# Seven block products for eight in two of eight pairs of the retention's projections

## The chip, the cores and the metric

The kernel runs on one core of one Trainium2 chip. The metric is device time in microseconds (us) of one execution. The kernel is compared with itself before one change.

## The reference

A trunk of two layers works on x of 256 positions by 2048 features, in float32. Layer 0 mixes with retention (8 heads), layer 1 with latent attention (16 heads); each is followed by a SwiGLU block of width 5632. Cut to what the change touches:

```
h    = rms_norm(x, norm_mix_pre[0])
proj = h @ ret_w_in                      # 2048 x 12288
q, k, v, g = split(proj, [2048, 4096, 8192])
q, k = rope(q), rope(k) * 256**-0.5      # 8 heads of 256
y    = retention(q, k, v)                # per head: (q k^T * decay) v
out  = silu(g) * group_norm(y) * gn_g    # 8 heads of 512
x    = x + rms_norm(out @ ret_w_out, norm_mix_post[0])
```

## The kernel before

**Tiles and products.** The 256 positions are two tiles of 128 (t = 0, 1). A projection is cut into groups of 1024 output columns, two halves of 512 (c = 0, 1), and its 2048 inputs into 16 slices of 128 (kt = 0 to 15). A group fills four PSUM banks b00, b01, b10, b11 (t, c). Each operand is kept as a high part (the value rounded to the fast matmul type) and a low part (the rest), and a product of two blocks is three matmuls of 128x128 by 512 columns: high by high, high by low, low by high. A slice of weights is loaded by one DMA of 512 KB (`raw`, 4 buffers); ScalarE casts the high part (L202), VectorE subtracts for the low part (L203), each 1024 wide (`whi`, `wlo`, 5 buffers each). PE may run at most as far as these buffers are filled.

**Sevens.** A pair p is the two slices 2p and 2p+1: a 2 by 2 block of inputs times a 2 by 2 block of weights, eight block products, 24 matmuls. For pairs in a list `sevens`, `group` forms them with seven products, 21 matmuls (Winograd's form of Strassen's method). That takes four sums of left blocks (`left_sums`, L229, formed once and used by all groups), four sums of weight blocks per group (`right_sums`, L237, tiles `ta` and `tb` with their own high and low parts `tahi`, `talo`, `tbhi`, `tblo`), and four more banks m1, m5, m6, m7. m1 and m6 come from the six banks for products, m5 and m7 are the two `misc` banks, which transposes, scores and head outputs also use. They gather over all pairs of the list. After the last such pair `combine` (L330) forms sums of them, and `add` (L341) adds these to the four banks, between the matmuls of later slices. Before the change, the gate/up groups (`gu`), the down projections (`dn`) and the retention's output projection (`rto`) have sevens.

**The retention.** Four query/key groups (rqk0 to rqk3, two heads each) are followed by eight value/gate groups (rvg0 to rvg7, one head each), all on the left operand `hT`, which `norm_piece` (L431) forms while rqk0 runs. After an rqk group VectorE turns the result (16 `rope` operations), PE transposes it (`rtp`) and forms scores (`rsc`), which VectorE multiplies with the decay (`pr`). After an rvg group the values are split (`vh`, `vl`); during the next group PE forms the head's output in a misc bank (`ry`, 3 matmuls for the first tile and 6 for the second), VectorE normalises it into `z` (L724 to L735), PE transposes z (`ztp`) and ScalarE writes it away (`yT`).

**What sets the order.** `later(k, fn)` puts work k steps ahead; a step is the load of one slice. Within that a scheduler orders the instructions of each engine; each engine then runs its own list in that order. Lists and waits are fixed when the program is built.

Of the kernel before, what the change touches and what calls it, by code (L numbers as in the profile page):

```python
# [8 lines left out]
F32 = mybir.dt.float32  # L9
F32R = mybir.dt.float32r  # L10
# [45 lines left out]
def trunk(  # L56
# [73 lines left out]
    def later(k, fn):  # L130
        order[0] += 1
        todo.append((steps[0] + k, order[0], fn))
# [125 lines left out]
    def group(  # L258
# [71 lines left out]
        def combine():  # L330
            def kept(n):
                return wp.tile([P, 512], F32, tag="mv", bufs=3, name=f"{name}_mv{n}")

            m1, u, v = kept(0), kept(1), kept(2)
            nc.scalar.copy(out=m1, in_=ms[1])
            nc.vector.tensor_add(out=u, in0=ms[6], in1=m1)
            nc.vector.tensor_add(out=v, in0=ms[7], in1=u)
            nc.vector.tensor_sub(out=u, in0=ms[5], in1=u)
            parts.update(m1=m1, u=u, v=v)

        def add(t, c):  # L341
            m1, u, v = parts["m1"], parts["u"], parts["v"]
            if (t, c) == (1, 1):
                nc.vector.tensor_sub(out=v, in0=ms[5], in1=v)
            src = {(0, 0): m1, (0, 1): u, (1, 0): v, (1, 1): v}[t, c]
            nc.vector.tensor_tensor(out=banks[t][c], in0=banks[t][c], in1=src, op=ALU.add)

        def adds(t):
# [57 lines left out]
    def tile_load(w, g, name, halves=0):  # L406

        def load(kt, first_half=False):  # L410
            n = 512 if kt < halves or first_half else 1024

            def dma(raw):
                for a in range(0, 1024, 512 if kt < halves else 1024):
                    m = 512 if kt < halves else 1024
                    nc.sync.dma_start(out=raw[:, a : a + m], in_=w[g, kt, :, a : a + m])

            parts = [(a, n, None) for a in range(0, 512 if first_half else 1024, n)]
            return weights(dma, parts, f"{name}_w{kt}")

        return load
# [5 lines left out]
    PIECES = ((0, 2), (2, 2), (4, 4), (8, 4), (12, 4))  # L427

    watch = [None]

    def norm_piece(t, i, ssq, col):  # L431
        k0, n = PIECES[i]
# [159 lines left out]
    def retention():  # L592
        first = [small(len(PIECES), "nxt", 4, f"first{t}") for t in range(NT)]

        def load_x(c, t):
            nc.sync.dma_start(
                out=xs[:, t, c * 512 : (c + 1) * 512], in_=xv[:, t, c * 512 : (c + 1) * 512]
            )

        def load_constants():  # L600
            nc.sync.dma_start(out=pos_i, in_=pos)
            nc.sync.dma_start(out=cst[:, 0:C_ID], in_=consts[:, 0:C_ID])
            nc.sync.dma_start(out=cst[:, C_MASK:C_DEC], in_=consts[:, C_MASK:C_DEC])

        load_x(0, 0)
        later(0, lambda: norm_piece(0, 0, first[0], G_MIX))
        later(0, lambda: norm_piece(0, 1, first[0], G_MIX))
# [11 lines left out]
        def qk_group(gq):  # L619
            name = f"rqk{gq}"  # L620
            return group(
                h_lhs, DT, tile_load(ret_qk, gq, name, 0 if gq else 1), name, lead=2 if gq else 3
            )

        def vg_group(h):
            name = f"rvg{h}"
            return group(h_lhs, DT, tile_load(ret_vg, h, name), name)

        with tc.tile_pool(name="rt_s", bufs=1) as sp:
            scores = {}  # L630
# [79 lines left out]
            with tc.tile_pool(name="rt_v", bufs=1) as rp:  # L710
                yT = rp.tile([P, RH * 4, NT, P], F32, name="yT")

                def mixed(h, t, pr, v, sg):
                    y = misc_bank(f"ry{h}{t}")

                    terms = [
                        (pr[a][:, (kb + t) * P : (kb + t + 1) * P], v[b][:, kb, :])
                        for kb in range(t + 1)
                        for a, b in ((0, 0), (0, 1), (1, 0))
                    ]  # L720
                    for n, (left, right) in enumerate(terms):
                        nc.tensor.matmul(y, left, right, start=n == 0, stop=n == len(terms) - 1)  # L722
                    st = rp.tile([P, 6], F32, tag="bst", bufs=4, name="bst")
                    nc.vector.bn_stats(out=st, in_=y)  # L724
                    mv = rp.tile([P, 2], F32, tag="bmv", bufs=4, name="bmv")
                    nc.vector.bn_aggr(out=mv, in_=st)
                    ve = rp.tile([P, 1], F32, tag="bve", bufs=4, name="bve")
                    nc.vector.tensor_scalar(ve, mv[:, 1:2], scalar1=EPS, scalar2=None, op0=ALU.add)
                    rs = rsqrt(ve, 1, "grs", 4, "grs")
                    z = rp.tile([P, RV], F32, tag="z", bufs=2, name="z")  # L730
                    nc.vector.scalar_tensor_tensor(
                        out=z, in0=y, scalar=mv[:, 0:1], in1=sg[:, t, :],
                        op0=ALU.subtract, op1=ALU.mult,
                    )
                    nc.vector.tensor_scalar(z, z, scalar1=rs, scalar2=None, op0=ALU.mult)  # L735

                    def transposes():
                        tp = misc_bank(f"ztp{h}{t}")
                        for j in range(4):
                            nc.tensor.transpose(  # L740
                                tp[:, j * P : (j + 1) * P], z[:, j * P : (j + 1) * P], ident
                            )
                        for j in range(4):
                            nc.scalar.activation(
                                out=yT[:, h * 4 + j, t, :], in_=tp[:, j * P : (j + 1) * P], func=AF.Copy,
                                scale=gain(G_GN, h * 4 + j),
                            )

                    later(4, transposes)

                for h in range(RH):
                    if h:
                        banks = vg_group(h)
                    vh = rp.tile([P, NT, RV], F32R, tag="vh", bufs=1, name=f"vh{h}")
                    vl = rp.tile([P, NT, RV], F32R, tag="vl", bufs=1, name=f"vl{h}")
                    ph = rp.tile([P, 3 * P], F32R, tag="ph", bufs=1, name=f"ph{h}")
                    pl = rp.tile([P, 3 * P], F32R, tag="pl", bufs=1, name=f"pl{h}")
                    split(ph, pl, scores[h])
                    sg = rp.tile([P, NT, RV], F32, tag="sg", bufs=1, name=f"sg{h}")
                    for t in range(NT):  # L760
                        split(vh[:, t, :], vl[:, t, :], banks[t][0], rx[t])
                        nc.scalar.activation(
                            out=sg[:, t, :], in_=banks[t][1], func=AF.Silu, scale=rx[t]
                        )
                    for t in range(NT):
                        later(2 + t, lambda h=h, t=t, pr=(ph, pl), v=(vh, vl), sg=sg: mixed(h, t, pr, v, sg))

                def sums():
                    both = ("vh", "vl")[sums.n % 2]
                    sums.n += 1  # L770
                    s = rp.tile([P, 2, 4, P], F32R, tag=both, bufs=1, name="rs")
                    f = rp.tile([P, 4, P], F32, tag="sg", bufs=1, name="rsf")
                    return f, s[:, 0], s[:, 1]

                sums.n = 0
                closing(
                    lambda k0, n: yT[:, k0 : k0 + n], RH * 4, ret_out, g_mix_post[0], G_FFN, "rto",
                    sevens=RTO_SEVENS, sums=sums,
                )


    def swiglu(i):
        with tc.tile_pool(name=f"ff{i}", bufs=1) as fp:
# [7 lines left out]
                    out=aT[:, j * 4 : j * 4 + 4, t, :], in_=tp.rearrange("p (j q) -> p j q", j=4)  # L791
                )


            ins = {}
            held = {}

            def sums(n=0):
                f = fp.tile([P, 4, P], F32, tag="sf", bufs=2, name=f"sf{i}")
                if n < 2:  # L800
                    hi = fp.tile([P, 4, P], F32R, tag="sa", bufs=4, name=f"sh{i}")
                    lo = fp.tile([P, 4, P], F32R, tag="sa", bufs=4, name=f"sl{i}")
                else:
                    hi = wp.tile([P, 4, P], F32R, tag="ah", bufs=3, name=f"sh{i}")
                    lo = wp.tile([P, 4, P], F32R, tag="al", bufs=3, name=f"sl{i}")
                return f, hi, lo

            def seen(t, k0, n, part):
                for p in GU_SEVENS:
                    if k0 <= 2 * p < k0 + n:  # L810
                        held[t, p] = part[:, 2 * p - k0], part[:, 2 * p - k0 + 1]
                        if (1 - t, p) in held:
                            f, hi, lo = sums(len(ins))
                            left_sums(*held[0, p], *held[1, p], f, hi, lo)
                            ins[p] = hi, lo
# [392 lines left out]
```

## Time and profile before

| | us |
|---|---|
| median of 3 runs | 2439.79 |
| lowest and highest run | 2439.47 to 2440.51 |
| the profiled execution | 2439.43 |
| its span, first to last instruction | 2437.6 |
| PE busy in it | 2425.1 |
| VectorE (DVE) busy | 1944.2 |
| ScalarE (ACT) busy | 1367.8 |

Times in the rows are microseconds from the span's start unless marked ns. PE is TensorE's matmuls, PEld its weight loads, DVE VectorE, ACT ScalarE, POOL GpSimd. A row's `x48` counts instructions. Buffer numbers are left out of names, so rvg_w_lo stands for the low parts of all value/gate groups.

### The profile page before, as it was taken

The numbers are of one execution on the slowest core, as the hardware profiler recorded it, in microseconds if no ns is written. First come the engines' busy times: TensorE is split into PE (matmuls) and PEld (weight loads), VectorE is DVE, ScalarE is ACT, GpSimd is POOL, SyncE is SP. The second block draws the span as 40 slices with busy tenths as digits, with TensorE's granted clock in tenths as the row PEclk, the third lists the DMA queues.
The fourth block names the chain that finished last, engine by engine and source line by source line (L and its number), as shares of the span: only waits on it lengthen the run. The fifth ranks groups of instructions, "written<-read, shape, count | busy, mean of one in ns | idle before, by whom it ended". The sixth has DMA issues, their size and how long they took to land.

```text
span 2437.6 us, 30634 instructions
## 1 busy us (share of the span) xinstructions
PE 2425.1 (99%) x11038; PEld 2005.3 (82%) x11038; DVE 1944.2 (80%) x2635; ACT 1367.8 (56%) x1825; POOL 25.0 (1%) x38
## 2 busy tenths in 40 slices
PE   9999999999999999999999999999999999999998
PEld 7888888888888888888888888888888888888887
DVE  7655555557888898898989997876789888899997
ACT  5433544445656555555566666655566555556664
POOL 0000000000000000000000000000000000000000
PEclk9999999999999999999999999999999999999999
DMA  7555555555656566565666565445556656566665
GB/s 263 180 185 182 180 182 180 181 179 178 200 199 201 179 200 209 188 207 181 209 199 206 193 212 160 131 134 190 189 179 201 209 187 202 185 207 203 199 197 165
DMA packets 129609, 463.75 MB, mean 190 GB/s; under 512 B 14640, under 2 KB 15024, under 8 KB 129456
## 3 DMA queue, kind: packets, MB, share of 16 engines
q1 hardware_dynamic: 129456, 461.80, 57.8%
q8 instruction: 86, 1.41, 0.2%
q14 instruction: 67, 0.55, 0.1%
HBM read 459.64 MB, written 2.10 MB: 189 GB/s over the span
## 4 chain that ended last, share of the span: by engine, by line
PE 98%; DVE 1%; DMA 1%; issue 0%; SPq 0%; ACT 0%; DVEq 0%; POOLq 0%; ACTq 0%
PE gu_b L399 30%; PE dn_b L399 16%; PE rvg_b L399 14%; PE rqk_b L399 7%; PE gu_m L399 6%; PE rto_b L399 6%; PE mlo_b L399 4%; PE q L399 3%; PE dn_m L399 3%; PE mc_b L399 2%; PE ftp L789 1%; PE rto_m L399 1%; PE ry L722 1%; PE htp L435 1%; PE asc L1048 0%; PE rsc L677 0%
## 5 line engine op out<-in xcount | busy, mean ns | idle before, releaser
L399 PE MATMUL gu_b<-gu_w_hi,hT 128*128 128x512 f32 x1976 | 570.5, 392 | 0.0
L202 ACT CAST gu_w_hi<-gu_w_raw 128x1024 fp32r<-128x1024 f32 (+1 forms) x352 | 340.7, 980 | 224.5 <-PE gu_b L399 141.6
L399 PEld LDWEIGHTS gu_b<-gu_w_hi,hT 128*128 128x128 f32 x1976 | 366.7, 188 | 75.2 <-DVE hT L203 0.9
L203 DVE TENSOR_TENSOR gu_w_lo<-gu_w_raw,gu_w_hi 128x1024 fp32r<-128x1024 f32 (+1 forms) x352 | 391.9, 1128 | 33.1 <-ACT gu_w_hi L202 30.9
L399 PE MATMUL gu_b<-gu_w_lo,hT 128*128 128x512 f32 x988 | 316.6, 390 | 0.0
L203 DVE TENSOR_TENSOR rvg_w_lo<-rvg_w_raw,rvg_w_hi 128x1024 fp32r<-128x1024 f32 x128 | 156.4, 1224 | 160.7 <-ACT rvg_w_hi L202 160.7
L399 PE MATMUL rvg_b<-rvg_w_hi,hT 128*128 128x512 f32 x1024 | 280.7, 391 | 0.0
L202 ACT CAST rvg_w_hi<-rvg_w_raw 128x1024 fp32r<-128x1024 f32 x128 | 135.0, 1054 | 195.6 <-PE rvg_b L399 187.2
L202 ACT CAST dn_w_hi<-dn_w_raw 128x1024 fp32r<-128x1024 f32 (+1 forms) x176 | 172.8, 993 | 98.5 <-DMA dn_w_raw<-w_down 45.1
L399 PEld LDWEIGHTS rvg_b<-rvg_w_hi,hT 128*128 128x128 f32 x1024 | 191.0, 188 | 38.9
L399 PEld LDWEIGHTS gu_b<-gu_w_lo,hT 128*128 128x128 f32 x988 | 185.2, 188 | 39.4 <-DVE gu_w_lo L203 0.6
L203 DVE TENSOR_TENSOR dn_w_lo<-dn_w_raw,dn_w_hi 128x1024 fp32r<-128x1024 f32 (+1 forms) x176 | 196.8, 1147 | 8.9 <-ACT dn_w_hi L202 8.6
L399 PE MATMUL dn_b<-dn_w_hi,dn_al 128*128 128x512 f32 x536 | 170.3, 389 | 0.0
L399 PE MATMUL dn_b<-dn_w_lo,dn_ah 128*128 128x512 f32 x536 | 170.2, 389 | 0.0
L399 PE MATMUL dn_b<-dn_w_hi,dn_ah 128*128 128x512 f32 x536 | 170.0, 390 | 0.0
L399 PE MATMUL rvg_b<-rvg_w_lo,hT 128*128 128x512 f32 x512 | 158.0, 390 | 0.0
L399 PE MATMUL rqk_b<-rqk_w_hi,hT 128*128 128x512 f32 x512 | 141.6, 394 | 2.2 <-ACT rqk_w_hi L202 1.4
L203 DVE TENSOR_TENSOR rqk_w_lo<-rqk_w_raw,rqk_w_hi 128x1024 fp32r<-128x1024 f32 (+1 forms) x65 | 77.5, 1207 | 59.0 <-ACT rqk_w_hi L202 58.9
L202 ACT CAST rqk_w_hi<-rqk_w_raw 128x1024 fp32r<-128x1024 f32 (+1 forms) x65 | 67.5, 1039 | 100.1 <-PE rqk_b L399 90.6
L399 PEld LDWEIGHTS dn_b<-dn_w_hi,dn_al 128*128 128x128 f32 x536 | 100.6, 188 | 21.0
L399 PEld LDWEIGHTS dn_b<-dn_w_lo,dn_ah 128*128 128x128 f32 x536 | 100.6, 188 | 20.9
L399 PEld LDWEIGHTS dn_b<-dn_w_hi,dn_ah 128*128 128x128 f32 x536 | 100.3, 188 | 20.6
(351 smaller groups left out, 4355.9 us busy)
## 6 DMA issues: line engine op xcount, KB each, us to landing
gu_w_raw<-w_gu SPq DMA_DIRECT2D x352, 512.0 KB, 4.2
dn_w_raw<-w_down SPq DMA_DIRECT2D x176, 512.0 KB, 4.4
rvg_w_raw<-ret_vg SPq DMA_DIRECT2D x128, 512.0 KB, 3.5
rto_w_raw<-ret_out SPq DMA_DIRECT2D x64, 512.0 KB, 4.2
rqk_w_raw<-ret_qk SPq DMA_DIRECT2D x63, 512.0 KB, 3.8
mlo_w_raw<-mla_out SPq DMA_DIRECT2D x32, 512.0 KB, 3.6
uq_w_raw<-mla_up SPq DMA_DIRECT2D x32, 448.0 KB, 3.4
mc_w_raw<-mla_c SPq DMA_DIRECT2D x16, 512.0 KB, 4.5
```

Source lines behind the costliest of these rows:

```text
L202: nc.scalar.copy(out=hi, in_=src)
L203: nc.vector.tensor_sub(out=lo, in0=src, in1=hi.bitcast(F32))
L399: nc.tensor.matmul(out, e[2](), e[3](), start=bank not in begun, stop=ends[bank, bank in added] == n, skip_group_check=bank in added,)
L435: nc.tensor.transpose(tp[:, j * P : (j + 1) * P], xs[:, t, (k0 + j) * P : (k0 + j + 1) * P], ident)
L722: nc.tensor.matmul(y, left, right, start=n == 0, stop=n == len(terms) - 1)
L789: nc.tensor.transpose(tp[:, b * P : (b + 1) * P], a[:, b * P : (b + 1) * P], ident)
```

## The change

`RET_SEVENS = (2, 4)`: pairs 2 and 4 (slices 4, 5 and 8, 9) of rqk1, rqk2, rqk3 and of all eight rvg groups are formed with seven products. rqk0 keeps eight, because the left sums are formed while it runs. `watched` is the code that formed the left sums for the gate/up groups, made a function of its own. `combine` now forms all four terms at once, the fourth in a buffer of its own (`x`, tag `tsum`), where `add` formed it late and in place; this holds for gu, dn and rto as well. The transposes of z are put 10 steps behind z, not 4.

```diff
+RET_SEVENS = (2, 4)
@@ combine, add
-            parts.update(m1=m1, u=u, v=v)
+            x = tp7.tile([P, 1024], F32, tag="tsum", bufs=2, name=f"{name}_mx")[:, 0:512]
+            nc.vector.tensor_sub(out=x, in0=ms[5], in1=v)
+            parts.update({(0, 0): m1, (0, 1): u, (1, 0): v, (1, 1): x})
 
         def add(t, c):
-            m1, u, v = parts["m1"], parts["u"], parts["v"]
-            if (t, c) == (1, 1):
-                nc.vector.tensor_sub(out=v, in0=ms[5], in1=v)
-            src = {(0, 0): m1, (0, 1): u, (1, 0): v, (1, 1): v}[t, c]
+            src = parts[t, c]
             nc.vector.tensor_tensor(out=banks[t][c], in0=banks[t][c], in1=src, op=ALU.add)
@@ before norm_piece
+    def watched(sevens, tiles):
+
+        made, held = {}, {}
+
+        def seen(t, k0, n, part):
+            for p in sevens:
+                if k0 <= 2 * p < k0 + n:
+                    held[t, p] = part[:, 2 * p - k0], part[:, 2 * p - k0 + 1]
+                    if (1 - t, p) in held:
+                        f, hi, lo = tiles(len(made))
+                        left_sums(*held[0, p], *held[1, p], f, hi, lo)
+                        made[p] = hi, lo
+
+        watch[0] = seen
+        return made
@@ retention
+        def tiles(n):
+            f, hi, lo = (
+                wp.tile([P, 4, P], d, tag=tag, bufs=3, name=f"rx{tag}")
+                for d, tag in ((F32, "ah"), (F32R, "ah"), (F32R, "al"))
+            )
+            return f, hi, lo
+
+        ins = watched(RET_SEVENS, tiles)
@@ qk_group, vg_group
-                h_lhs, DT, tile_load(ret_qk, gq, name, 0 if gq else 1), name, lead=2 if gq else 3
+                h_lhs, DT, tile_load(ret_qk, gq, name, 0 if gq else 1), name, lead=2 if gq else 3,
+                sevens=RET_SEVENS if gq else (), left=lambda p: ins[p],
-            return group(h_lhs, DT, tile_load(ret_vg, h, name), name)
+            return group(
+                h_lhs, DT, tile_load(ret_vg, h, name), name, sevens=RET_SEVENS, left=lambda p: ins[p]
+            )
@@ mixed
-                    later(4, transposes)
+                    later(10, transposes)
@@ swiglu
-            ins = {}
-            held = {}
-            def seen(t, k0, n, part):
...
-            watch[0] = seen
+            ins = watched(GU_SEVENS, sums)
```

In the lists that follow, numbers in names only tell buffers apart. First PE, at slice 4 of rvg3. Before, the first slice of pair 2 is twelve matmuls:

```order
L399 MATMUL rvg3_b00_2733<-rvg3_w4_hi_2844,hT_90 128x512
L399 MATMUL rvg3_b01_2734<-rvg3_w4_hi_2844,hT_90 128x512
L399 MATMUL rvg3_b00_2733<-rvg3_w4_lo_2845,hT_90 128x512
L399 MATMUL rvg3_b01_2734<-rvg3_w4_lo_2845,hT_90 128x512
L399 MATMUL rvg3_b00_2733<-rvg3_w4_hi_2844,hT_90 128x512
L399 MATMUL rvg3_b01_2734<-rvg3_w4_hi_2844,hT_90 128x512
```

Six like these follow for b10 and b11, and slice 5 takes twelve more. Now PE has this at the same place, where `rxah` and `rxal` are the high and low parts of the left sums:

```order
L399 MATMUL rvg3_m1_3120<-rvg3_w4_hi_3096,hT_90 128x512
L399 MATMUL rvg3_m1_3120<-rvg3_w4_lo_3097,hT_90 128x512
L399 MATMUL rvg3_m1_3120<-rvg3_w4_hi_3096,hT_90 128x512
L399 MATMUL rvg3_b00_2985<-rvg3_w5_hi_3102,hT_90 128x512
L399 MATMUL rvg3_b00_2985<-rvg3_w5_lo_3103,hT_90 128x512
L399 MATMUL rvg3_b00_2985<-rvg3_w5_hi_3102,hT_90 128x512
L399 MATMUL rvg3_b01_2986<-rvg3_w5_hi_3102,rxah_220 128x512
L399 MATMUL rvg3_b01_2986<-rvg3_w5_lo_3103,rxah_220 128x512
L399 MATMUL rvg3_b01_2986<-rvg3_w5_hi_3102,rxal_221 128x512
L399 MATMUL rvg3_m5_3122<-rvg3_w2_tahi_3112,rxah_220 128x512
L399 MATMUL rvg3_m5_3122<-rvg3_w2_talo_3113,rxah_220 128x512
L399 MATMUL rvg3_m5_3122<-rvg3_w2_tahi_3112,rxal_221 128x512
```

Three matmuls each for m7, m6 and b10 follow, 21 for the pair; m5 and m7 need the misc banks in which `ry` of the head before stood.

Second VectorE, at the start of rvg3, from the statistics of head 2's first tile on, before:

```order
L724 BN_STATS bst_2777<-ry20_2773 128x6
L203 TENSOR_TENSOR rvg3_w6_lo_2881<-rvg3_w6_raw_2878,rvg3_w6_hi_2880 128x1024
L726 BN_AGGR bmv_2779<-bst_2777 128x2
L728 TENSOR_SCALAR bve_2781<-bmv_2779 128x1
L731 SCALAR_TENSOR_TENSOR z_2785<-ry20_2773,bmv_2779,sg2_2726 128x512
L735 TENSOR_SCALAR z_2785<-z_2785,grs_2783 128x512
L203 TENSOR_TENSOR rvg3_w7_lo_2908<-rvg3_w7_raw_2905,rvg3_w7_hi_2907 128x1024
L724 BN_STATS bst_2813<-ry21_2806 128x6
L203 TENSOR_TENSOR pl3_3079<-pr11_1081,ph3_3078 128x384
L726 BN_AGGR bmv_2815<-bst_2813 128x2
L728 TENSOR_SCALAR bve_2817<-bmv_2815 128x1
L731 SCALAR_TENSOR_TENSOR z_2821<-ry21_2806,bmv_2815,sg2_2726 128x512
```

And now, from z of the first tile on:

```order
L758 SCALAR_TENSOR_TENSOR z_3037<-ry20_3025,bmv_3031,sg2_2978 128x512
L762 TENSOR_SCALAR z_3037<-z_3037,grs_3035 128x512
L204 TENSOR_TENSOR rvg3_w2_tblo_3117<-rvg3_w2_tb_3107,rvg3_w2_tbhi_3116 128x1024
L751 BN_STATS bst_3065<-ry21_3058 128x6
L247 TENSOR_TENSOR rvg3_w4_ta_3193<-rvg3_w8_raw_3181,rvg3_w9_raw_3187 128x512
L753 BN_AGGR bmv_3067<-bst_3065 128x2
L248 TENSOR_TENSOR rvg3_w4_tb_3194<-rvg3_w4_ta_3193,rvg3_w9_raw_3187 128x512
L755 TENSOR_SCALAR bve_3069<-bmv_3067 128x1
L758 SCALAR_TENSOR_TENSOR z_3073<-ry21_3058,bmv_3067,sg2_2978 128x512
L249 TENSOR_TENSOR rvg3_w4_tb_3194<-rvg3_w4_tb_3194,rvg3_w9_raw_3187 128x512
L762 TENSOR_SCALAR z_3073<-z_3073,grs_3071 128x512
L204 TENSOR_TENSOR rvg3_w6_lo_3148<-rvg3_w6_raw_3145,rvg3_w6_hi_3147 128x1024
```

Sums of pair 4, from the weights of slices 8 and 9, stand between the statistics and z of the second tile, and the low part of slice 6 stands behind z. Ahead of these rows, as the change has it, come the two `vl`, the low parts of slices 4 and 5, two sums of pair 2, the statistics of the first tile, talo and one sum of pair 4.

Third VectorE, where rqk0 ends and rqk1 begins, before:

```order
L203 TENSOR_TENSOR rqk1_w1_lo_609<-rqk1_w1_raw_606,rqk1_w1_hi_608 128x1024
L703 TENSOR_SCALAR rope_c_102<-cos_t_79,first_r0_r_508 128x128
L703 TENSOR_SCALAR rope_c_102<-cos_t_79,first_r1_r_514 128x128
L203 TENSOR_TENSOR rqk1_w2_lo_645<-rqk1_w2_raw_642,rqk1_w2_hi_644 128x1024
L203 TENSOR_TENSOR rqk1_w3_lo_675<-rqk1_w3_raw_672,rqk1_w3_hi_674 128x1024
L643 TENSOR_TENSOR rope_a_559<-rqk0_b00_104,rope_c_102 128x512
```

And now:

```order
L246 TENSOR_TENSOR rqk1_w2_ta_734<-rqk1_w4_raw_708 128x512
L730 TENSOR_SCALAR rope_c_102<-cos_t_79,first_r0_r_526 128x128
L730 TENSOR_SCALAR rope_c_102<-cos_t_79,first_r1_r_532 128x128
L204 TENSOR_TENSOR rqk1_w2_lo_663<-rqk1_w2_raw_660,rqk1_w2_hi_662 128x1024
L247 TENSOR_TENSOR rqk1_w2_ta_734<-rqk1_w4_raw_708,rqk1_w5_raw_728 128x512
L248 TENSOR_TENSOR rqk1_w2_tb_735<-rqk1_w2_ta_734,rqk1_w5_raw_728 128x512
L670 TENSOR_TENSOR rope_a_577<-rqk0_b00_104,rope_c_102 128x512
```

Three sums of pair 2 have moved ahead of the rope operations, which read rqk0's banks, and slice 3's low part behind them.

## Rows read from the trace of the kernel before

**Rows 1.** The page: its head, and part 1.

```profile
span 2437.6 us, 30634 instructions
PE 2425.1 (99%) x11038; PEld 2005.3 (82%) x11038; DVE 1944.2 (80%) x2635; ACT 1367.8 (56%) x1825; POOL 25.0 (1%) x38
```

**Rows 2.** Waits of PE: who for whom, us in total, times, longest.

```profile
PE gu_m L399 <- DVE gu_w_tblo L203: 0.4, 1, 0.4
```

**Rows 3.** The chain in order of time: start us, us, engine, line, count.

```profile
367.01 27.25 PE rvg_b L399 x120
...
413.56 27.25 PE rvg_b L399 x120
...
825.93 18.36 PE gu_b L399 x81
...
868.61 18.36 PE gu_b L399 x81
```

**Rows 4.** Stretches: length, busy us of each engine, PEclk, DMA share, GB/s.

```profile
core 0: us, PE busy (x) PEld busy (x) DVE busy (x) ACT busy (x) POOL busy (x), PEclk, DMA share, GB/s
...
116.00:164.00 48.00, 48.00 (x226) 40.14 (x225) 27.69 (x35) 18.85 (x22) 0.00 (x0) 1.00 0.56 184
...
351.80:398.30 46.50, 46.50 (x210) 38.47 (x210) 25.32 (x30) 21.83 (x30) 1.09 (x2) 1.00 0.53 181
...
859.50:902.20 42.70, 42.70 (x193) 35.08 (x192) 38.74 (x49) 24.33 (x28) 0.00 (x0) 1.00 0.61 197
```

**Rows 5.** Groups of instructions: busy us, mean ns; the last row has least/median/most ns.

```profile
L203 DVE TENSOR_TENSOR rvg_w_lo<-rvg_w_raw,rvg_w_hi 128x1024 fp32r<-128x1024 f32 x128 | 156.4, 1224 | 160.7 <-ACT rvg_w_hi L202 160.7
...
L203 DVE TENSOR_TENSOR gu_w_tblo<-gu_w_tb,gu_w_tbhi 128x1024 fp32r<-128x1024 f32 x60 | 73.5, 1225 | 36.7 <-ACT gu_w_tbhi L202 34.3
...
L346 DVE TENSOR_TENSOR gu_b<-gu_b,gu_mv 128x512 f32<-128x512 f32 x80 | 53.8, 696 | 6.0 <-PE gu_b L399 6.0
...
L202 ACT CAST gu_w_tahi<-gu_w_ta 128x1024 fp32r<-128x1024 f32 x60 | 63.2, 1054 | 27.5 <-DVE gu_w_ta L246 14.8 <-PE gu_b L399 12.5 <-ACT gu_w_hi L202 0.2
...
L246 DVE TENSOR_TENSOR gu_w_ta<-gu_w_raw 128x512 f32<-128x512 f32 x60 | 41.2, 687 | 16.6 <-DMA gu_w_raw<-w_gu 16.5
...
L231 DVE TENSOR_TENSOR sf<-hx x6: 283/284/288, 764.1 to 1743.9; 128x128 f32<-128x128 f32 x6
```

**Rows 6.** Timeline at an rvg group's start: start us, us; VectorE, ScalarE, then PE.

```profile
389.36 0.75 DVE L206 SCALAR_TENSOR_TENSOR vl<-rvg_b,first_r_r,vh 128x512 fp32r<-128x512 f32 x1 [0.24 <-ACT vh L205]
...
392.94 1.05 ACT L202 CAST rvg_w_hi<-rvg_w_raw 128x1024 fp32r<-128x1024 f32 x1 [2.10 <-PE rvg_b L399]
394.30 1.06 ACT L202 CAST rvg_w_hi<-rvg_w_raw 128x1024 fp32r<-128x1024 f32 x1 [0.30 <-PE rvg_b L399]
397.70 1.05 ACT L202 CAST rvg_w_hi<-rvg_w_raw 128x1024 fp32r<-128x1024 f32 x1 [2.34 <-PE rvg_b L399]
...
394.10 0.39 PE L722 MATMUL ry<-vh,ph 128*128 128x512 f32 x1
```

**Rows 7.** Timeline around rope operations: the first and last of 16, rvg0's first matmuls.

```profile
200.82 0.68 DVE L643 TENSOR_TENSOR rope_a<-rqk_b,rope_c 128x512 f32<-128x512 f32 x1
...
207.95 0.42 DVE L649 TENSOR_TENSOR rope_o<-rope_b,rope_a 128x256 f32<-128x256 f32 x1
...
201.11 0.62 PE L399 MATMUL rvg_b<-rvg_w_hi,hT 128*128 128x512 f32 x2
...
160.34 4.63 DVE L203 TENSOR_TENSOR rqk_w_lo<-rqk_w_raw,rqk_w_hi 128x1024 fp32r<-128x1024 f32 x4
```

**Rows 8.** Timeline where rqk0 ends: VectorE, then PE.

```profile
55.86 1.22 DVE L203 TENSOR_TENSOR rqk_w_lo<-rqk_w_raw,rqk_w_hi 128x1024 fp32r<-128x1024 f32 x1 [1.50 <-ACT rqk_w_hi L202]
57.00 0.68 DVE L643 TENSOR_TENSOR rope_a<-rqk_b,rope_c 128x512 f32<-128x512 f32 x1
...
56.79 1.07 PE L399 MATMUL rqk_b<-rqk_w_hi,hT 128*128 128x512 f32 x4
```

**Rows 9.** A DMA issue's median us to landing, and VectorE's waits for such loads.

```profile
rvg_w_raw<-ret_vg SPq DMA_DIRECT2D x128, 512.0 KB, 3.5
...
DVE gu_w_ta L246 <- DMA gu_w_raw<-w_gu: 16.5, 19, 1.1
```

More of the change, by code (lines that the diff above doesn't have):

```diff
@@ L806, in sums @@
                 return f, hi, lo
-            def seen(t, k0, n, part):
[L809 to L815, printed above, removed]
-            watch[0] = seen
+            ins = watched(GU_SEVENS, sums)
             for j in range(FF // 512):
```

## The prediction

> **What bounds the kernel now.** I read the page's busy shares first, then PE's own waits, then the chain of waits in order of time, and last the stretches. PE is busy for 2425.1 us of the span of 2437.6 us [rows 1]. A busy PE alone proves little, because matmul ends are modelled, so the next view counts more: after the start-up PE waited for another engine once, 0.4 us for a VectorE result in a gate/up group [rows 2]. [...] The rvg group has 192 + 9 matmuls of 512 columns and 8 transposes, the gate/up group, which already does seven products for eight in three pairs, has 183 and 8 transposes. [...]
>
> **What is removed.** The change puts two pairs on seven products in 3 of the 4 query/key groups (rqk1 to rqk3) and all 8 rvg groups. A pair had 8 block products of 3 matmuls and now has 7, so a group loses 2 x 3 = 6 and the kernel 11 x 6 = **66 matmuls**: 66 x 0.227 = **15.0 us**, all of it on the path, since PE is the path. [...] The trace has 227 ns, and that decides.
>
> **What is added beside it.** VectorE, for each pair: four 512-wide sums (0.687 us each), two 1024-wide low parts (1.225), and one 1024-wide low part (1.224) shrinks to half, about 0.6 less [rows 5]: 4.6 us. For each group: four forming operations and four adds at 0.696: 5.6 us [rows 5]. Together 2 x 4.6 + 5.6 = **14.8 us a group**. An rvg group has 25.3 us of VectorE work in 46.5 us and a query/key group 27.7 in 48.0 [rows 4]; they would have 40 in 45.2 and 42.5 in 46.6, shares of 0.89 and 0.91. The gate/up group runs with 38.7 in 42.7, also 0.91 [rows 4], and there PE's only wait was 0.4 us. ScalarE gets four casts of 1.054 [rows 5], one 512-wide copy, and loses two half casts: some 4 us on 22 in 46.5 [rows 4], no bound. No DMA and nothing on POOL is added. So on average the cover is there; what can fail is the order within a group, which I follow at three places, with 1.14 us from start to start for a 1024-wide VectorE operation (four in 4.63 us [rows 7]) and about 0.60 for a 512-wide one.
>
> *Entry of an rvg group.* Let 0 be the group's first matmul; the first ry matmul of the head before stands 24 matmuls later, so 0 is 394.10 - 5.44 = 388.66 [rows 6]. VectorE's second vl ends at 1.4 [rows 6]; then a sum, the half w4_lo, a sum (3.2); w5_lo waits for its cast, which ScalarE can start at 392.94, that is 4.3, when PE gives back the buffer [rows 6]: it ends at 6.5. The statistics of ry0, talo (its cast starts at 394.30, 5.6, in time), a sum, z and its scaling end near 10.5; tblo waits for a cast that starts at 397.70, 9.0 [rows 6], and ends at 11.6; then the statistics of ry1, two sums and z: 14.4. This last z frees the second misc bank, for which m7 asks after 69 matmuls, at 15.6: **1.2 us to spare**. w6_lo is ready at 16.6 and asked for after 80 matmuls, at 18.1: 1.5 to spare. The chained product tblo of pair 4 has about 1.1.
>
> *Entry of a query/key group and of rvg0.* The 16 rope operations start 0.3 us before the group's first matmul and take 7.5 us [rows 7]; w4_lo, w5_lo and three sums bring VectorE to 10.7; the casts of ta, tb and w6 stand behind ScalarE's four copies of the transposes (near 11.1), so talo, tblo and w6_lo end at 13.3, 14.5 and 15.6, and the two score multiplications that free the misc banks at 16.1 and 16.6. PE asks for these at 17.2 and 17.9. Again 1.1 to 1.3 us to spare.
>
> *rqk0 to rqk1, once.* Before, VectorE idles 1.50 us ahead of the last low part, and the rope operations start at 57.00, 0.25 us before rqk1's first matmul, the third of the four that start at 56.79 [rows 8]. Now the left sums of both pairs (eight operations of 0.284, two low parts of about 0.7 [rows 5]) fall into rqk0, more than that idle time hides, and three sums stand ahead of the rope operations, two of them waiting for weights that land about 3.5 us after issue (the figure of rvg loads, the nearest [rows 9]). I expect the rope operations about 1 us later: rqk1's fourth bank 0.3 us late and the m banks up to 0.8 us late. I charge **0.7 us**; bounds 0 and 2.
>
> The transposes of z move from 4 to 10 steps behind z: the same 8 a group, now ahead of kt 13 and 14 instead of 7 and 8, because m5 and m7 hold both misc banks from kt 5 to 9; z has two buffers and the next is written some 5 steps later, so nothing waits. The four-in-one combine moves one VectorE operation a group earlier in gate/up, down and rto groups and frees a misc bank some 4 kts sooner; PE waits for neither today, so I cost it at nothing, bounds -0.4 (the one wait there is) and +0.4.
>
> **Sum.** 2439.43 us (the profiled execution; span 2437.6) - 15.0 + 0.7 = 2425.1. The median stands 0.36 above that execution, so **2425.5 us**. For what the trace doesn't show, the ends are no further loss and a loss of 0.4 us, the one wait of PE on VectorE there is, in each of the 10 other groups, 4 us; I take no loss, since the spare times are all above 1 us.
>
> **Rivals.** *VectorE late in every group.* If my spare times of 1.2 us are wrong by 1.2 to 2.2 us, PE loses 0 to 1 us in each of 11 groups: 2425 to 2436; at the middle, 0.5, 2430.3. For it: shares of 0.9 and long in-order queues. Against: the gate/up groups with the same share.
>
> *Slower.* Place: the sum of pair 4's second tile (ta from w9's raw weights) stands in VectorE's queue ahead of the z that frees the misc bank for m7. [...] w9's load goes out when w5_lo is done, at 6.5, and VectorE reaches that sum near 12.2. A load that takes over 5.7 us holds z up, one over 6.9 holds PE, and above 8.3 each group gives back more than its 6 x 0.227 = 1.36 us. At 9.1 us PE loses 2.2 in each of 11 groups: 2425.5 + 24 = 2449.7, slower. For it: sums of this kind do wait for loads in gate/up groups, 16.5 us in 19 times. Against: the longest was 1.1, and the median landing is 3.5 us with DMA engines about half busy [rows 4, 9].
>
> *PE is not the bound.* [...] If VectorE's 80% set the pace, 66 fewer matmuls would bring nothing: 2439.8. [...]
>
> **Chances.** Forecast (2424 to 2428) 0.68; VectorE late by up to 0.9 us a group (2428 to 2435) 0.20; nothing left of the gain within 4.9 us, by either rival, 0.07; slower 0.05. About 0.2%, 4.9 us, is what a measurement of this kernel tells from no change. Faster by more 0.88, within 0.07, slower by more 0.05. The range goes from 2424.0, the whole gain with a little scatter, to 2433, most of the first rival.
>
> **What would show it.** Right: 66 matmul records fewer on line 399; rvg periods of 45.2 and query/key periods of 46.6 us; VectorE at 0.9 there; PE's waits unchanged but for about 1 us near 60 to 76 us. Wrong: waits of m5, m7 or w6's first product on z, pr or w_lo in every group, or longer periods than these. A matmul on the m banks costing other than 0.227 us would also break the sum.

## The result, and the profile after

| | before | after |
|---|---|---|
| median, four runs each | 2439.63 | 2426.81 |
| lowest and highest run | 2438.60 to 2440.51 | 2426.16 to 2426.96 |
| ratio to before, 95% interval | | 0.9947 [0.9930, 0.9964] |
| span of the profiled execution | 2437.6 | 2425.2 |

The change makes the kernel 12.8 us faster, 0.53%. Forecast were 14.3 us less, at 2425.5. In a second series the changed kernel had a median of 2426.14 beside 2440.10 before it, 14.0 us less.

The page's head and part 1 (busy us, share of the span, instructions), to be set beside [rows 1], and all waits of PE for others (us, times, longest), beside [rows 2]:

```profile
span 2425.2 us, 30883 instructions
...
PE 2412.2 (99%) x10972; PEld 1993.3 (82%) x10972; DVE 2080.2 (86%) x2865; ACT 1409.8 (58%) x1882; POOL 26.2 (1%) x38
```

```profile
PE warm L97 <- DVE mhalf L113: 1.2, 1, 1.2
PE rqk_b L399 <- ACT rqk_w_hi L203: 0.9, 1, 0.9
PE htp L451 <- DMA xs<-x: 0.9, 2, 0.7
PE rqk_b L399 <- DVE rqk_w_lo L204: 0.2, 1, 0.2
PE rqk_b L399 <- ACT hT L203: 0.2, 1, 0.2
```

66 matmuls are gone (11038 to 10972 records). VectorE does 230 operations and 136 us more, and all five waits of PE are of the start-up: none is in a group with the new sevens.

The chain of waits in order of time (start us, us, engine, line, count), two stretches of the query/key groups and two of the rvg groups, the ones between left out. First two of the query/key groups before, 47.95 us apart, then the kernel after:

```profile
111.69 2.75 PE rqk_b L399 x12
...
159.64 2.75 PE rqk_b L399 x12
```

```profile
77.52 6.12 PE rqk_b L399 x27
...
124.12 6.12 PE rqk_b L399 x27
...
351.83 6.12 PE rvg_b L399 x27
...
397.02 6.12 PE rvg_b L399 x27
```

The periods, from a place in one group to the same place in the next, are 124.12 - 77.52 = **46.60** and 397.02 - 351.83 = **45.19 us**: to a hundredth what 6 matmuls less give (forecast 46.6 and 45.2; before 47.95 for query/key and 46.55 for rvg [rows 3]). VectorE in such a query/key and such an rvg group (stretch, length, busy us of each engine, clock, DMA share, GB/s; beside [rows 4]):

```profile
77.50:124.10 46.60, 46.60 (x220) 38.99 (x219) 39.97 (x54) 22.56 (x26) 0.00 (x0) 1.00 0.59 190
...
351.80:397.00 45.20, 45.20 (x205) 37.39 (x204) 37.39 (x50) 25.62 (x35) 1.10 (x2) 1.00 0.58 187
```

Where the rest went is seen by cutting both traces at the same instructions of PE (times read from PE's timeline; spans are read to 0.1 us, so the last row and the sum are good to 0.05):

| stretch of the trace | before | after | difference |
|---|---|---|---|
| start, to the last transposes of h in rqk0 | 40.02 | 40.74 | +0.72 |
| retention, from there to the first matmul of rto | 534.83 | 519.86 | **-14.97** |
| rto and gate/up of layer 0 | 648.12 | 648.19 | +0.07 |
| down projection of layer 0, to the first matmul of layer 1 | 232.61 | 233.49 | +0.88 |
| from there to the start of the last matmul | 973.61 | 973.49 | -0.12 |
| from there to the end of the span | 8.41 | 9.43 | +1.02 |
| sum | 2437.6 | 2425.2 | -12.4 |

The retention gives the whole 66 x 0.227 = 15.0 us. Three stretches outside it give 2.6 us back: the start, layer 0's down projection, the end. The experiments ask which of these belong to the change, how near VectorE is to its limit, and whether a third pair pays.

### The profile page after: what moved, and what is told of

The parts are those of the page before. It is cut to its first block, busy times and chain, and to the rows that moved or that the text cites. A ratio compares the mean times of both kernels' runs of the same rounds, so it can differ in the third digit from the quotient of the medians.

```text
span 2425.2 us, 30883 instructions
## 1 busy us (share of the span) xinstructions
PE 2412.2 (99%) x10972; PEld 1993.3 (82%) x10972; DVE 2080.2 (86%) x2865; ACT 1409.8 (58%) x1882; POOL 26.2 (1%) x38
## 3 DMA queue, kind: packets, MB, share of 16 engines
q8 instruction: 86, 1.41, 0.2%
## 4 chain that ended last, share of the span: by engine, by line
PE 96%; DVE 2%; DMA 1%; issue 1%; ACT 0%; SPq 0%; DVEq 0%; POOLq 0%; POOL 0%; ACTq 0%
PE gu_b L399 31%; PE dn_b L399 14%; PE rvg_b L399 12%; PE gu_m L399 7%; PE rto_b L399 6%; PE rqk_b L399 6%; PE mlo_b L399 4%; PE q L399 3%; PE dn_m L399 2%; PE rvg_m L399 2%; PE mc_b L399 2%; PE ftp L816 1%; PE rqk_m L399 1%; PE rto_m L399 1%; PE ry L749 1%; PE htp L451 1%
## 5 line engine op out<-in xcount | busy, mean ns | idle before, releaser
L399 PE MATMUL gu_b<-gu_w_hi,hT 128*128 128x512 f32 x1976 | 564.0, 392 | 0.0
L399 PE MATMUL gu_b<-gu_w_lo,hT 128*128 128x512 f32 x988 | 310.1, 390 | 0.0
L399 PE MATMUL rvg_b<-rvg_w_hi,hT 128*128 128x512 f32 x800 | 227.0, 391 | 0.0
L203 ACT CAST rvg_w_hi<-rvg_w_raw 128x1024 fp32r<-128x1024 f32 (+1 forms) x128 | 127.3, 1000 | 117.6 <-PE rvg_b L399 93.6
L204 DVE TENSOR_TENSOR rvg_w_lo<-rvg_w_raw,rvg_w_hi 128x1024 fp32r<-128x1024 f32 (+1 forms) x128 | 145.2, 1154 | 36.1 <-ACT rvg_w_hi L203 34.9
L399 PEld LDWEIGHTS rvg_b<-rvg_w_hi,hT 128*128 128x128 f32 x800 | 149.0, 188 | 30.3
L399 PE MATMUL rvg_b<-rvg_w_lo,hT 128*128 128x512 f32 x400 | 124.8, 390 | 0.0
L399 PE MATMUL rqk_b<-rqk_w_hi,hT 128*128 128x512 f32 x428 | 121.0, 394 | 1.1 <-ACT rqk_w_hi L203 0.9
L203 ACT CAST gu_w_tbhi<-gu_w_tb 128x1024 fp32r<-128x1024 f32 x60 | 63.1, 1052 | 86.7 <-DVE gu_w_tb L249 47.4
L204 DVE TENSOR_TENSOR gu_w_tblo<-gu_w_tb,gu_w_tbhi 128x1024 fp32r<-128x1024 f32 x60 | 73.5, 1225 | 36.8 <-ACT gu_w_tbhi L203 34.3
```

Source lines behind the costliest of these rows:

```text
L203: nc.scalar.copy(out=hi, in_=src)
L204: nc.vector.tensor_sub(out=lo, in0=src, in1=hi.bitcast(F32))
L399: nc.tensor.matmul(out, e[2](), e[3](), start=bank not in begun, stop=ends[bank, bank in added] == n, skip_group_check=bank in added,)
```

## The experiments

All were timed beside the kernel before on the same chip. One table has the stretches of each trace (us; "late" marks the kernels in which gate/up, rto and dn form the fourth term late and in place, as before), and the median of the runs with its ratio to before:

| kernel | start | retention | layer 0's dn | end | median, ratio |
|---|---|---|---|---|---|
| before, first trace | 40.02 | 534.83 | 232.61 | 8.41 | 2439.63 |
| before again | 40.34 | 534.82 | 232.61 | 8.45 | 2440.13, 1.0000 [0.9992, 1.0009] |
| new terms alone | 40.70 | 534.83 | 232.89 | 8.58 | 2441.17, 1.0003 [0.9995, 1.0012] |
| after, first trace | 40.74 | 519.86 | 233.49 | 9.43 | 2426.81, 0.9947 [0.9930, 0.9964] |
| after again | 39.70 | 519.86 | 233.21 | 9.34 | 2426.14, 0.9942 [0.9929, 0.9954] |
| after, fourth late | 40.11 | 519.96 | 232.67 | 8.45 | 2424.39, 0.9935 [0.9922, 0.9949] |
| the same again, late | 39.56 | 519.86 | 233.48 | 8.47 | 2425.15, 0.9936 [0.9923, 0.9950] |
| two more operations | 39.76 | 519.86 | 233.03 | 8.42 | 2425.95, 0.9946 [0.9932, 0.9960] |
| three more operations | 39.54 | 519.98 | 232.78 | 8.47 | 2425.18, 0.9944 [0.9931, 0.9956] |
| eight more operations | 40.70 | 521.18 | 232.96 | 8.48 | 2432.79, 0.9971 [0.9960, 0.9982] |
| pairs 2, 3, 4, late | 40.97 | 519.52 | 232.62 | 8.49 | 2425.66, 0.9943 [0.9930, 0.9955] |
| the same in rvg alone, late | 40.62 | 519.97 | 232.61 | 8.49 | 2425.26, 0.9940 [0.9928, 0.9953] |
| pairs 2, 4, 5, late | 40.09 | 524.25 | 232.62 | 8.41 | 2426.68, 0.9947 [0.9935, 0.9960] |
| the same in rvg alone, late | 39.15 | 522.20 | 232.61 | 8.47 | 2426.64, 0.9951 [0.9939, 0.9964] |

### Both kernels again

No edit. Of before:

> The kernel before, unchanged, to learn how much two executions of one kernel differ at the places where the changed kernel was later than the sum (start of the long run of matmuls in the first query/key group at 41.06 us; first matmul of layer 1's first projection; 3.5 us from the last update of x to the end of the span). Theory 'scatter': the start moves by up to 0.7 us and the end by up to 1 us with nothing changed. Rival 'the change costs it': both come out as in the first trace within 0.1 us. Time 2439.5 within 1 us by both.

Of the changed kernel:

> The changed kernel, unchanged. Forecast of the sum 2425.5; first measured 2426.8. Theory 'scatter': at the start and at the end this trace differs from the first one of the changed kernel by as much as the two kernels did (0.7 and 1.0 us), while the loss at the two ends of a down-projection half (0.32 and 0.63 us) comes back. Rival 'systematic': all four come back within 0.1 us. Group periods 45.19 and 46.60 us by both.

The start is scatter: 40.02 and 40.34 before, 40.74 and 39.70 after, and 39.15 to 40.97 over all fourteen traces, with no order by kernel. The retention repeats to 0.01 us in each of the two kernels. The end came back longer in both traces of the changed kernel (9.43 and 9.34), and in no other trace, not even in those with the same code behind the retention (two, three and eight more operations). There the last of the output's eight stores landed in 3.4 us; elsewhere the slowest took 2.5 to 2.7. From layer 1 on, the lists of PE, VectorE and ScalarE in those three traces, and in that of the new terms alone, are the same operation for operation. So no code of the change stands behind it, but why it came twice in one kernel stays open.

### The new terms alone

```diff
-RET_SEVENS = (2, 4)
+RET_SEVENS = ()
```

> No sevens in the retention; only the terms formed all at once and the later transposes of z are kept. Theory A (forming the fourth term at once puts one VectorE operation ahead of low parts in the down projections, and near their ends VectorE is what PE waits for): about 0.95 us slower than before, 0.3 at the end of the first half of layer 0's down projection and 0.6 at the first group of layer 1; 2440.5. Rival B (as the sum had it, it costs nothing): 2439.5 and these places as in the kernel before within 0.1 us. Later transposes of z: 0 by both.

The retention is as before (534.83), so the later transposes of z cost nothing. Layer 0's down projection lost 0.28 us of the 0.95 that theory A gave. 2441.17 against 2440.10 leans to theory A; its interval holds no difference.

### The fourth term late in gate/up, rto and dn

```diff
-            parts.update({(0, 0): m1, (0, 1): u, (1, 0): v, (1, 1): x})
+            parts.update({(0, 0): m1, (0, 1): u, (1, 0): v, (1, 1): v})
+            if name[:2] in ("gu", "dn") or name[:3] == "rto":
+                return
...
+            if (t, c) == (1, 1) and (name[:2] in ("gu", "dn") or name[:3] == "rto"):
+                nc.vector.tensor_sub(out=src, in0=ms[5], in1=src)
```

> The changed kernel, but in the gate/up groups and the output and down projections the fourth term is formed late and in place as before; the retention keeps the new form. Theory A: the 0.95 us of the down projection come back, the wait of 0.4 us in a gate/up group too; 1.0 us below the changed kernel at the first group of layer 1 (15.0 less than before but for the start): 2425.5 to 2426. Rival B (these 0.95 us are no matter of the fourth term): as the changed kernel, 2426.8.

Repeated:

> The run with the fourth term late in the gate/up, output and down groups once more, to see what of its lead over the changed kernel (2424.4 against 2426.1 in the same call) comes back. Theory A: layer 0's down projection loses under 0.1 us between its first matmul and the first group of layer 1, against 0.88 and 0.60 in the two traces of the changed kernel. If the last store of the output lands in 2.7 us again, against 3.4 in both traces of the changed kernel, the end belongs to it too; if it takes 3.4, that is scatter. Time 2424 to 2425.5.

In the first trace the down projection lost 0.06 us, in the second 0.87, as much as the changed kernel. So theory A doesn't explain all of it. The two losses are different waits, though. In the second trace PE waited 0.6 us for a `dn_w_tblo` in the middle of a half; "three more operations" has such a wait, 0.6 us, in layer 1. At the *end* of the down projection all six traces with the new terms are later than all eight with the old: from the first transposes of layer 1 to its first matmul 3.34 to 3.44 us against 3.18 or 3.19. VectorE's timeline there, first in the changed kernel (start us, us, engine, line, operation, in brackets idle time before it and its releaser):

```profile
1421.30 0.68 DVE L341 TENSOR_TENSOR dn_mx<-dn_m,dn_mv 128x512 f32<-128x512 f32 x1
...
1426.72 4.81 DVE L204 TENSOR_TENSOR dn_w_lo<-dn_w_raw,dn_w_hi 128x1024 fp32r<-128x1024 f32 x4
...
1434.28 1.22 DVE L204 TENSOR_TENSOR mc_w_lo<-mc_w_raw,mc_w_hi 128x1024 fp32r<-128x1024 f32 x1 [1.19 <-ACT mc_w_hi L203]
1435.42 1.17 DVE L204 TENSOR_TENSOR kr_w<-kr_raw,kr_w 128x64 fp32r<-128x64 f32 x8
1436.51 0.15 DVE L556 TENSOR_REDUCE dn_s<-dn_ssq 128x1 f32<-128x3 f32 x1
...
1440.42 0.75 DVE L457 TENSOR_TENSOR hx<-htp,gcol 128x256 f32<-128x256 f32 x2
```

and with the fourth term late:

```profile
1425.77 0.69 DVE L350 TENSOR_TENSOR dn_mv<-dn_m,dn_mv 128x512 f32<-128x512 f32 x1
1426.38 1.22 DVE L204 TENSOR_TENSOR dn_w_lo<-dn_w_raw,dn_w_hi 128x1024 fp32r<-128x1024 f32 x1
...
1431.79 1.22 DVE L204 TENSOR_TENSOR mc_w_lo<-mc_w_raw,mc_w_hi 128x1024 fp32r<-128x1024 f32 x1
1432.93 1.84 DVE L204 TENSOR_TENSOR kr_w<-kr_raw,kr_w 128x64 fp32r<-128x64 f32 x13
1434.69 0.15 DVE L561 TENSOR_REDUCE dn_s<-dn_ssq 128x1 f32<-128x3 f32 x1
...
1439.01 0.74 DVE L462 TENSOR_TENSOR hx<-htp,gcol 128x256 f32<-128x256 f32 x2
```

In the first, the low part of layer 1's first weights waits 1.19 us for its cast, and the closing operations of the down projection, which lead over `xs` and `hx` to layer 1's first products, stand behind it in VectorE's queue. Up to the down projection the first trace is 0.53 us behind the second (1208.79 against 1208.26 at its first matmul); that low part comes 2.49 us later in it, `dn_s` 1.82, `hx` 1.41 and layer 1's first matmul 1.35. The cast waits for a load, and the chain of the changed kernel (start us, us, what) shows what that waited for, a `dn_w_lo` of VectorE:

```profile
1426.80 1.15 DVE dn_w_lo L204
1427.96 5.16 DMA mc_w_raw<-mla_c
1433.16 0.04 issue
1433.20 1.06 ACT mc_w_hi L203
```

All four adds and the early fourth term stand ahead of that low part in VectorE's list. With the fourth term late only two adds do, and SyncE issues the load 3.3 us sooner, 2.7 without the 0.53:

```profile
1424.69 0.33 SPq L421 DMA_DIRECT2D mc_w_raw<-mla_c  x1
```

So the early term costs 0.16 to 0.26 us at layer 1's entry in every trace that has it. The other 0 to 0.6 us of the down projection comes and goes: with the early term it came in four traces of six, with the late one in one of eight, there 0.87 us. This version has the lowest medians, 15.7 us below before in both series, but its interval overlaps that of the changed kernel, and part of its lead over it is the last store.

### More work for VectorE

```diff
                     z = rp.tile([P, RV], F32, tag="z", bufs=2, name="z")
+                    for _ in range(2 if t else 0):      # then 3, then 8
+                        nc.vector.tensor_tensor(out=z, in0=y, in1=sg[:, t, :], op=ALU.mult)
```

> The changed kernel with two needless 512-wide VectorE operations (0.60 us each from start to start) ahead of the last z of each head; z is written by them first and then rightly. In the order of VectorE one of them takes the place of a sum that moves behind z, so z comes 0.6 us later. In the trace of the changed kernel z leaves the misc bank 1.55 us before m7 asks for it. Theory 'spare time at the entry': 0.95 us are left, nothing is lost: 2426 to 2427, rvg period 45.19. Rival 'VectorE at its limit' (every operation counts): 8 x 1.2 = 9.6 us slower, 2436.

> The same with three such operations. Now the low part of slice 6 (1.14 us) comes to stand ahead of z too, so z is 3 x 0.60 + 1.14 = 2.94 us later than in the changed kernel and 1.4 us later than m7 asks for the bank. Theory 'spare time at the entry': PE waits about 1.4 us in each of the groups rvg1 to rvg7, about 10 us, with 1.4 us more if the output projection's start suffers too: 2436 to 2438, rvg period 46.6. Rival 'the average share decides' (VectorE would be busy 39.2 of 45.2 us): nothing lost, 2426.5.

Two more: nothing is lost, as the spare time at the entry has it, and the rival falls. Three more: expected were 1.4 us a group, measured 0.02 (retention 519.98 against 519.86, period 45.19). The theory of spare time, read as a fixed distance, falls here. PE's timeline at the place:

```profile
394.36 0.39 PE L399 MATMUL rvg_m<-rvg_w_tbhi,rxah 128*128 128x512 f32 x1
...
395.72 0.39 PE L399 MATMUL rvg_b<-rvg_w_hi,hT 128*128 128x512 f32 x1
395.95 0.39 PE L399 MATMUL rvg_m<-rvg_w_tahi,rxah 128*128 128x512 f32 x1
```

m6 (`tbhi`) runs first, then a product of slice 6, then m7 (`tahi`) at 395.95; z has let go of the bank at 395.00 + 0.74 = 395.74:

```profile
395.00 0.74 DVE L760 SCALAR_TENSOR_TENSOR z<-ry,bmv,sg 128x512 f32<-128x512 f32 x1
```

Counted from the group's first matmul, at 378.72, z is done at 17.0 us, 2.9 later than in the changed kernel and as late as expected. But m7 asks at 17.2 and no longer at 15.6. The lists were ordered anew with the three operations in them, and m7 went behind products that were ready: what PE wanted next had itself moved with VectorE's lateness.

> The changed kernel with eight needless 512-wide VectorE operations ahead of the last z of each head, 4.8 us a group; VectorE would be busy 37.4 + 4.8 = 42.2 of 45.2 us, 0.93, about as with a third pair (41.5 of 44.5). With three such operations nothing was lost, since the order of PE moved too: m7's products stood behind the next ones. Theory 'a share of VectorE up to 0.9 and a little more costs nothing': rvg period within 0.2 us of 45.19, time 2426 to 2428. Rival 'VectorE gives out at this share': the period grows by 0.4 us or more as with the third pair, 3 to 10 us slower.

With eight more VectorE is busy 41.97 of 45.38 us, 0.92, and the period grows by 0.19 us: the first theory, at its edge. But the kernel is 7.1 us below before instead of 14.0, outside that theory's 2426 to 2428. Most of the difference lies behind the retention: the left sums of rto stand behind the last head's z, and PE waited for them once:

```profile
PE rto_b L399 <- ACT rs L203: 4.0, 1, 4.0
```

### A third pair

```diff
-RET_SEVENS = (2, 4)
+RET_SEVENS = (2, 3, 4)      # then (2, 4, 5); each also in the rvg groups alone
@@ tiles of the left sums: a buffer more
-                for d, tag in ((F32, "ah"), (F32R, "ah"), (F32R, "al"))
+                for d, tag in ((F32, "mv"), (F32R, "ah"), (F32R, "al"))
```

> Pairs 2, 3 and 4 on seven products in the retention, the fourth term late in the other groups as in the run before. 33 matmuls fewer again, 33 x 0.227 = 7.5 us, if PE sets the pace: rvg period 44.5, query/key period 45.9, time 2424.4 - 7.5 = 2416.9. VectorE would then be busy 37.4 + 4.1 = 41.5 of 44.5 us in an rvg group and 40.4 + 4.1 = 44.5 of 45.9 in a query/key group (0.93 and 0.97). Rival 'the entry decides': pair 3 wants its sums and low parts, 4.1 us of VectorE work, some 7 us after m7 asks for its bank, and with 1.0 to 1.5 us to spare there PE waits 1 to 2 us in every group: 11 to 22 us back, 2428 to 2439, slower than with two pairs.

> The third pair in the eight rvg groups only; the query/key groups keep two. 24 matmuls fewer, 5.4 us. If PE sets the pace 2419.0, rvg period 44.5. If the entry of a group decides, 1 to 2 us are lost in each of the eight: 2427 to 2435. Against the run with three pairs everywhere it tells in which kind of group VectorE gives out first.

> Pairs 2, 4 and 5 on seven products in the retention, the fourth term late in the other groups. 33 matmuls fewer than with two pairs. With pairs 2, 3 and 4 an rvg group took 44.95 us, 0.24 less than with two pairs and 0.44 more than its matmuls; PE waited 0.7 us for ScalarE's casts of pair 4's sums. If the loss comes from three pairs in a row at the group's start, where VectorE also has the last head's work, the period is now 44.5 (query/key 45.9) and the time 2424.4 - 7.5 = 2417 to 2419. If it comes from VectorE's share, which is the same, 44.95 again and the time 2424 to 2426.

> The third pair (5) in the eight rvg groups only. 24 matmuls fewer than with two pairs: 2419.0 at most, rvg period 44.5, if the place of the pair was what cost; 2424 to 2426 with a period of 44.95 if it was VectorE's share.

None brings the 5.4 or 7.5 us below the two pairs with the fourth term late (2424.39 and 2425.15). With pairs 2, 3, 4 an rvg period is 44.95 us: 0.24 of the 0.68 us are gained, and the first and last groups give that back. PE's weight loads in such a group of the run in rvg alone, with VectorE's sums and ScalarE's casts before them:

```profile
403.78 0.30 PEld L404 LDWEIGHTS rvg_m<-rvg_w_tahi,rxah 128*128 128x128 f32 x2 [0.51 <-ACT rvg_w_tahi L203]
...
405.21 0.19 PEld L404 LDWEIGHTS rvg_m<-rvg_w_tbhi,rxah 128*128 128x128 f32 x1 [0.21 <-ACT rvg_w_tbhi L203]
```

```profile
401.88 0.69 DVE L247 TENSOR_TENSOR rvg_w_ta<-rvg_w_raw 128x512 f32<-128x512 f32 x1
```

```profile
402.68 1.05 ACT L203 CAST rvg_w_tahi<-rvg_w_ta 128x1024 fp32r<-128x1024 f32 x1 [2.84 <-DVE rvg_w_ta L247]
```

VectorE, behind the low parts of pairs 3 and 4, forms `ta` of pair 4 at 401.88; ScalarE, idle for 2.84 us, casts it until 403.73; PE asked 0.51 us earlier. Pairs 2, 4, 5 should have left VectorE room. They do worse: periods from 44.8 to 46.5 us in rvg, and in one trace 48.6 ahead of rto. In the run in rvg alone VectorE waits 1.42 us for a load before a sum of pair 5. The rest of that pair's work stands behind that sum with hardly a gap, and PE waits 1.65 us for its last low part:

```profile
401.74 0.69 DVE L247 TENSOR_TENSOR rvg_w_ta<-rvg_w_raw 128x512 f32<-128x512 f32 x1 [1.42 <-DMA rvg_w_raw<-ret_vg]
...
407.81 1.22 DVE L204 TENSOR_TENSOR rvg_w_tblo<-rvg_w_tb,rvg_w_tbhi 128x1024 fp32r<-128x1024 f32 x1
```

```profile
409.08 0.50 PE L404 MATMUL rvg_m<-rvg_w_tblo,rxah 128*128 128x512 f32 x1 [1.65 <-DVE rvg_w_tblo L204]
```

That load took 5.3 us. One group earlier the same sum waited 0.35 us, PE did not wait, and the period is 44.80. In the two traces PE waits for this low part nine times, and each time that sum had waited for its load, 0.5 to 2.3 us. In the query/key groups pairs 2, 4, 5 do better: periods of 46.17 us against 46.35 or more with pairs 2, 3, 4, where the matmuls alone would give 45.9.

So neither of the two theories had it alone. VectorE's share is 0.89 to 0.94 in the rvg groups of all four runs. With pairs 2, 3, 4 most of them lose 0.4 us; with pairs 2, 4, 5 they lose 0.3 when the loads land in time, up to 2.0 when that load is late, and 4.1 once, ahead of rto. Of the sets tried, two pairs are what the retention carries. With eight more operations the share was as high and the loss 0.19; what differs in the traces is the waits for casts and loads, but no run tests that alone.

## Why the prediction was right, point by point

- **PE as the bound, 0.227 us a matmul.** Right: 14.97 us of 15.0 in three of the four traces with this retention, 14.87 in the other. The price is the trace's own row, 27.25 / 120 us a matmul [rows 3] at a granted clock of 1.00 [rows 4], and the periods of the kernel before, 46.55 us for rvg and 42.68 for gate/up [rows 3], bear it out: they differ by 3.9 us, where 18 matmuls less make 4.1. After the change 27 matmuls took 6.12 us, 0.227 each, in a query/key and in an rvg group alike. The rival of no gain, 2439.8, fell: the median is 2426.81.
- **VectorE's added work, 14.8 us a group.** Too much: an rvg group has 37.39 us instead of 25.32 [rows 4], 12.1 more, a share of 0.83 and not 0.89 (query/key 0.86, not 0.91). The step took durations; neighbours overlap, and start to start a 512-wide operation takes 0.60 us, not 0.687. By those prices, which the prediction used for the entry, the sum is 2 x 4.1 + 8 x 0.60 = 13.1. Added up one by one, the durations in the two rvg stretches do grow by the 14.8 (from 26.07 to 40.87); busy time grows less, because the denser list overlaps more. Two neighbours of the changed kernel, 0.60 apart:

```profile
382.58 0.68 DVE L248 TENSOR_TENSOR rvg_w_tb<-rvg_w_ta,rvg_w_raw 128x512 f32<-128x512 f32 x1
383.18 0.69 DVE L204 TENSOR_TENSOR rvg_w_lo<-rvg_w_raw,rvg_w_hi 128x512 fp32r<-128x512 f32 x1
```

- **The entry of an rvg group.** In rvg4 the first matmul is at 385.29 - 5.44 = 379.85. These are the last rows of VectorE ahead of w6's low part, and PE's first matmul of m7:

```profile
391.88 0.68 DVE L247 TENSOR_TENSOR rvg_w_ta<-rvg_w_raw 128x512 f32<-128x512 f32 x1
...
393.20 0.74 DVE L758 SCALAR_TENSOR_TENSOR z<-ry,bmv,sg 128x512 f32<-128x512 f32 x1
...
394.85 4.09 DVE L204 TENSOR_TENSOR rvg_w_lo<-rvg_w_raw,rvg_w_hi 128x1024 fp32r<-128x1024 f32 x4
```

```profile
395.49 0.39 PE L399 MATMUL rvg_m<-rvg_w_tahi,rxah 128*128 128x512 f32 x1
```

  z lets go of the bank at 393.94, 14.1 us into the group (worked out: 14.4), and m7 asks at 15.6 (15.6): 1.55 us to spare against 1.2. The slower rival's sum runs at 12.0 us (12.2) and waits for nothing, though loads land in 4.4 us now, not 3.5. Right, but the spare time was taken as a fixed distance, and the run with three more operations shows that it is not. The slower rival's mechanism exists all the same: with pair 5 a sum that waited 1.42 us for its load held up VectorE's list, and PE behind it for 1.65 us.
- **The entry of a query/key group.** Right, with more room: in the group that starts at 104.6 us the second score multiplication ends at 120.75, and m7 asks for its bank at 122.59, 1.8 us later (worked out: 1.3).

```profile
119.73 1.02 DVE L709 TENSOR_TENSOR pr<-rsc,dec 128x384 f32<-128x384 f32 x2
...
122.59 0.39 PE L399 MATMUL rqk_m<-rqk_w_tahi,rxah 128*128 128x512 f32 x1
```

- **rqk0 to rqk1, 0.7 us.** Wrong, it cost 0.00 (22.67 us from the last transposes of h to the first of q and k, before and after). The rope operations start at 57.37, which is 57.00 [rows 8] plus the later start of 0.72 less 0.35: slice 3's low part, which had its idle time in front, went behind them, and that made up for the sums. The order shown ahead of the prediction has that move; the step counted the sums alone. With a third pair (2, 4, 5) the place does cost 0.9 us.
- **The four-in-one combine, nothing with bounds of 0.4.** Too small: 0.16 to 0.26 us at layer 1's entry in every trace that has it, 0.17 to 0.88 in the whole down projection. The step looked for PE's waits at the groups' ends; the price came over VectorE's queue, a low part waiting for a cast ahead of the closing operations. The wait of 0.4 us in a gate/up group [rows 2] is gone, but it is back with the new terms alone, so the early term did not remove it.
- **The start and the end.** Not in the sum: +0.72 and +1.02 us in this trace, scatter of the start and one slow store. The 0.7 charged for rqk0 happened to cover the first, which was luck. The second trace of the changed kernel is 14.5 us shorter than the second of before (2423.5 and 2438.0), with 14.3 forecast.
- **VectorE late in every group.** Didn't come: PE has no wait in these groups. It shows at a share of 0.92, with eight more operations or a third pair, and not yet at 0.87, with three. The middle of this rival, 2430.3, is a slip: 2425.5 and 5.5 make 2431.0.

## What to carry to other kernels

Here, with PE busy for 99% of the span, 66 matmuls taken away gave 14.97 us, 0.227 us each, their pitch in the trace. What was lost with more work on VectorE did not follow its share alone: at shares of 0.89 to 0.94 a group lost 0.19 us with eight more operations and 0.3 to 4.1 with a third pair, where PE waited for casts and, behind late loads, for low parts. Follow the entry of a group on VectorE's queue, start to start. Spare time there was no fixed distance, because the scheduler ordered the lists anew (three more operations were to cost 1.4 us a group and cost 0.02), so measure it by adding work. And look for the price of a moved operation where its engine's queue ends in a chain (a norm, the next layer's input; here 0.16 to 0.26 us at layer 1's entry), not only where it stands.

## What the runs showed of the hardware

- **The start.** Fourteen traces reach the last transposes of h in rqk0 39.15 to 40.97 us after the first instruction. From 8 to 14 us, between PE's waits for loads of x and for casts, the mean granted clock was 0.72 in both traces of before and in the first of after, 1.00 in the second of after (39.70) and in the earliest (39.15), 0.50 in the latest (40.97).
- **A wait that costs more than itself.** In the run with eight more operations PE stood still for 4.0 us, and the output projection took 180.7 us instead of 173.9, 6.8 more. Its stretch after the wait (length, busy us, the clock third from the end):

```profile
585.40:588.00 2.60, 2.56 (x6) 2.04 (x7) 1.83 (x6) 0.80 (x2) 0.00 (x0) 0.50 0.03 6
588.00:591.00 3.00, 3.00 (x9) 2.33 (x9) 2.86 (x7) 1.89 (x3) 0.00 (x0) 0.56 0.00 0
591.00:594.00 3.00, 3.00 (x15) 2.49 (x14) 3.00 (x4) 2.97 (x4) 0.00 (x0) 1.00 0.74 247
```

  The granted clock was 0.50 and 0.56 in the 5.6 us after the wait and 1.00 in the next stretch, and matmuls stood 0.43 us apart from 586.03 to 590.30 instead of 0.227. It fell after shorter waits, too: with pairs 2, 4, 5, in the period of 48.6 us, PE stood still for 0.4 and 1.5 us within 2.7 us, and in the stretch that follows the clock was 0.50. In the group with the single wait of 1.65 us, in the run in rvg alone, its mean was 1.00.

```profile
548.00:551.30 3.30, 3.30 (x9) 2.59 (x8) 3.30 (x5) 1.04 (x1) 0.00 (x0) 0.50 0.41 148
```

- **Loads.** The median rvg load lands in 4.4 us instead of 3.5 at a DMA share of 0.58 instead of 0.53, with the same bytes in less time (187 GB/s instead of 181 in the two rvg stretches).
